# Loading the first part of a tuned matmul as float32 through SyncE, with nine warm matmuls for sixteen, and cutting k in three parts

## Chip, cores, metric

One core of one Trainium2 chip. The metric is device time in microseconds of one execution; the median of several executions is quoted. The profile's *span* runs from the first to the last instruction and is 1.7 to 3.0 us shorter than the time of the same execution, so spans are compared with spans and times with times.

## The reference

```python
m, k, n = 4096, 4096, 4096          # a, b, bias: float32, normal
return np.tanh(np.matmul(a, b) + bias)
```

## The kernel before

A and B are float32 in HBM, and TensorE multiplies float16. GpSimd's DMA queue casts on the way in. The output has four column blocks of 1024. For each row tile of 128 and column half of 512, TensorE adds up 32 k tiles of 128. Nothing is loaded at the start, so the first 8 row tiles go through the first column block in two groups of four, and k is cut in parts: group 0 and then group 1 do k tiles 0 to 7, their sums are set aside in SBUF ("spill"), and then both do the rest. Until the data is there, TensorE multiplies zeros ("warm") to raise its clock: in the trace its weight loads stand 0.43 us apart up to 5.08 us, and the matmuls 0.215 us apart in the steady part.

In the code, `across` goes through the k tiles and takes all row tiles at each, `down` finishes one row tile after the other, and a "turn" transposes A. In the profile lines `nat` is A as loaded, `tp` its transposes in PSUM, `at` and `atx` the turned A of group 0 and of group 1, `an` the A that VectorE turns itself, and `ps` the sums.

```python
    WARM = 16
    ...
    for i in range(WARM):
        nc.tensor.matmul(warm, zeros[:, :P], zeros, start=i == 0, stop=i == WARM - 1)

    raw_b = spill[3].rearrange("P (t x) n -> P t (x n)", t=2)[:, ds(0, 1), :]
    load_b_low(nc.sync, raw_b, 0, 0, 1)                   # B, k tile 0: float32, SyncE
    nc.scalar.copy(b_cur[0][:, 0, :], raw_b[:, 0, :])     # rounded by ScalarE
    nat = [opool.tile([P, P, KS], fp16, name=f"nat_{m}", tag="o_sb") for m in range(G)]

    def load_nat(m):                                      # A, row tile m: cast by GpSimd's queue
        nc.gpsimd.dma_start(
            out=nat[m], in_=a[ds(m * P, P), ds(0, P * KS)].rearrange("m (x t) -> m x t", t=KS)
        )
    ...
    def turn_nat(m):
        tp = psum.tile([P, KS, P], fp16, name="tp", tag="ps")
        for t in range(KS):
            nc.tensor.transpose(tp[:, t, :], nat[m][:, :, t], ident)
        h = KS // 2
        nc.vector.tensor_copy(ats[m][:, ds(0, h), :], tp[:, ds(0, h), :])
        nc.scalar.copy(ats[m][:, ds(h, h), :], tp[:, ds(h, h), :])
    ...
    turn_nat(0)
    turn_nat(1)
    row(0, 0, 1)      # 2 matmuls: row tile 0, k tile 0, both column halves
    row(1, 0, 1)
    across(ps, (0, 1), 1, 1, 0)
    turn_nat(2)
    ...
    across(ps, range(G), 3, KS - 2 - 3, 0)
    ...
    down(ps, KS - 2, KS, put_aside0)
    ...
    group1(0, KS, put_aside1, before1)
    # then group 0 with k tiles 8 to 31, then group 1 with k tiles 8 to 31
```

Of the kernel before, what the change touches and what calls it, by code (L numbers as in the profile page):

```python
# [14 lines left out]
P = 128  # L15
Q = 4
QP = 32
NB = 512
fp32 = mybir.dt.float32
# [4 lines left out]
def kernel(  # L24
# [7 lines left out]
    nc = tc.nc  # L32
# [4 lines left out]
    KT = K // P  # L37
    MT = M // P
    NCW = 1024
    NC = N // NCW  # L40
    J = NCW // NB
    TB = 4
    G = 4
    KS = 8
    AN = 3
    WARM = 16

    singles = ctx.enter_context(tc.tile_pool(name="singles", bufs=1))
    bpool = ctx.enter_context(tc.tile_pool(name="bpool", bufs=2))
    anat = ctx.enter_context(tc.tile_pool(name="anat", bufs=AN))  # L50
# [8 lines left out]
    def new_b():  # L59
        return [  # L60
            bpool.tile([P, TB, NCW], fp16, name=f"b_{i}", tag=f"b_{i}") for i in range(KT // TB)
        ]

    def load_b_low(queue, dst, n0, t0, nt):

        src = b[ds(0, P * KS), ds(n0, NCW)].rearrange("(x t) n -> x t n", t=KS)
        queue.dma_start(out=dst, in_=src[:, ds(t0, nt), :])  # L67
# [32 lines left out]
    def load_bias(bias_bc, n0, queue):  # L100
        src = bias[ds(n0, NCW)]
        queue.dma_start(
            out=bias_bc,
            in_=bass.AP(tensor=src.tensor, offset=src.offset, ap=[[0, P], *src.ap]),
        )


    queue, live, staged = [], [0], {}

    def pump():  # L110
        while queue and (queue[0][0] is None or live[0] < AN):
            key, uses, load = queue.pop(0)
            made = load()
            if key is not None:
                live[0] += 1
                staged[key] = [made, uses]

    def want_a(key, uses, *where):
        queue.append((key, uses, lambda: load_a(*where)))

    def want(load):
        queue.append((None, 0, load))

    def turn(at, key, mb0, t0, nt):
        pump()
        transpose_a(at, staged[key][0], mb0, t0, nt)
        staged[key][1] -= 1
        if not staged[key][1]:
            live[0] -= 1
            pump()  # L130
# [6 lines left out]
    def finish(ps, addend, mi, c0, w=NB, o_sb=None, queues=(nc.sync,)):  # L137
# [17 lines left out]
    b_cur = new_b()  # L155
    spill = [
        bpool.tile([P, 4, NB], fp32, name=f"spill_{i}", tag=f"b_{i}") for i in range(2 * G * J // 4)
    ]
    ats = [atp.tile([P, KT, P], fp16, name="at") for m in range(G)] + [
        bpool.tile([P, KT, P], fp16, name=f"atx_{m}", tag=f"b_{4 + m}") for m in range(G)  # L160
    ]

    def aside(m, j):
        return spill[(m * J + j) // 4][:, (m * J + j) % 4, :]

    def put_aside0(ps, m, j):
        nc.scalar.copy(aside(m, j), ps)  # L167

    def add_bias(m, j):
        nc.vector.tensor_tensor(  # L170
            out=aside(m, j), in0=aside(m, j), in1=bias_bc[:, ts(j, NB)], op=mybir.AluOpType.add
        )

    def put_aside1(ps, m, j):
        nc.vector.tensor_tensor(  # L175
            out=aside(m, j), in0=ps, in1=bias_bc[:, ts(j, NB)], op=mybir.AluOpType.add
        )

    def end(ps, m, j):
# [2 lines left out]
    def banks():  # L182
        return [[psum.tile([P, NB], fp32, name="ps") for j in range(J)] for m in range(G)]

    def load_b_all(t0, nt):
        for q in (0, 2, 1, 3):
            load_b(b_cur, 0, t0, nt, q)

    def across(ps, ms, t0, nt, first):
        for t in range(t0, t0 + nt):  # L190
            for m in ms:
                for j in range(J):
                    mm(ps[m][j], ats[m], b_cur, t, j, t == first, False)

    def down(ps, t0, t1, done):
        for m in range(G):
            for j in range(J):
                for t in range(t0, t1):
                    mm(ps[m][j], ats[m], b_cur, t, j, False, t == t1 - 1)
                done(ps[m][j], m, j)  # L200

    def group1(t0, t1, done, before):
        for m in range(G, 2 * G):
            for j in range(J):
                ps = psum.tile([P, NB], fp32, name="ps")
                for t in range(t0, t1):
                    mm(ps, ats[m], b_cur, t, j, t == t0, t == t1 - 1)
                before(m, j)
                done(ps, m, j)
# [6 lines left out]
    warm = psum.tile([P, NB], fp32, name="ps")  # L216
    for i in range(WARM):
        nc.tensor.matmul(warm, zeros[:, :P], zeros, start=i == 0, stop=i == WARM - 1)  # L218



    raw_b = spill[3].rearrange("P (t x) n -> P t (x n)", t=2)[:, ds(0, 1), :]
    load_b_low(nc.sync, raw_b, 0, 0, 1)
    nc.scalar.copy(b_cur[0][:, 0, :], raw_b[:, 0, :])


    nat = [opool.tile([P, P, KS], fp16, name=f"nat_{m}", tag="o_sb") for m in range(G)]

    def load_nat(m):
        nc.gpsimd.dma_start(  # L230
            out=nat[m], in_=a[ds(m * P, P), ds(0, P * KS)].rearrange("m (x t) -> m x t", t=KS)
        )

    def load_b_next():
        t = b_done[0]
        b_done[0] += 1
        load_b_low(nc.gpsimd, b_cur[t // TB][:, ds(t % TB, 1), :], 0, t, 1)

    def turn_nat(m):
        tp = psum.tile([P, KS, P], fp16, name="tp", tag="ps")  # L240
        for t in range(KS):
            nc.tensor.transpose(tp[:, t, :], nat[m][:, :, t], ident)  # L242
        h = KS // 2
        nc.vector.tensor_copy(ats[m][:, ds(0, h), :], tp[:, ds(0, h), :])  # L244
        nc.scalar.copy(ats[m][:, ds(h, h), :], tp[:, ds(h, h), :])

    b_done = [1]
    load_nat(0)
    load_nat(1)
    nc.gpsimd.affine_select(  # L250
        out=ident, in_=ident, compare_op=mybir.AluOpType.is_equal, fill=0.0,
        base=0, pattern=[[-1, P]], channel_multiplier=1,
    )
    load_b_next()
    for m in (2, 3):
        load_nat(m)
        load_b_next()
    while b_done[0] < KS:
        load_b_next()
    want_a("g1a", 2, 4 * P, 2 * Q, 0, KS)  # L260
    bias_bc = biasp.tile([P, NCW], fp32, name="bias_bc")
    want(lambda: load_bias(bias_bc, 0, nc.gpsimd))
    want_a("g1b", 2, 6 * P, 2 * Q, 0, KS)
    SA = [(KS, 8), (16, 6), (22, 6), (28, 4)]
    SB = [[(8, 4), (12, 4)], [(16, 4), (20, 2)], [(22, 2), (24, 4)], [(28, 4)]]
    for (t, nt), bs in zip(SA, SB):
        want_a(("g0", t), G, 0, G * Q, t, nt)
        for u, nu in bs:
            want(lambda u=u, nu=nu: load_b_all(u, nu))
    SG = [[(KS, 12), (KS + 12, KT - KS - 12)]] + [[(KS, KT - KS)]] * (G - 1)  # L270
    for m in range(G):
        for t, nt in SG[m]:
            want_a(("g1", m, t), 1, (G + m) * P, Q, t, nt)
    todo = [(c, mi) for c in range(NC) for mi in range(MT) if (c, mi) >= (0, 2 * G)]

    ps = []

    def row(m, t0, nt):
        if len(ps) == m:
            ps.append([psum.tile([P, NB], fp32, name="ps") for j in range(J)])  # L280
        across(ps, (m,), t0, nt, 0)

    turn_nat(0)
    turn_nat(1)
    row(0, 0, 1)
    row(1, 0, 1)
    across(ps, (0, 1), 1, 1, 0)
    turn_nat(2)
    row(2, 0, 2)
    across(ps, (0, 1, 2), 2, 1, 0)  # L290
    turn_nat(3)
    row(3, 0, 3)
    across(ps, range(G), 3, KS - 2 - 3, 0)

    def turn1(m):
        turn(ats[G + m], "g1a" if m < 2 else "g1b", (m % 2) * Q, 0, KS)

    turn1(0)
    turn1(1)
    down(ps, KS - 2, KS, put_aside0)  # L300


    def turn0(i, m):
        turn(ats[m], ("g0", SA[i][0]), m * Q, *SA[i])

    def before1(m, j):
        if m < 6 and j == 0:
            turn1(m - 2)
        if m == 6:
            turn0(0, j)  # L310
        if m == 7:
            turn0(0, 2 + j)

    group1(0, KS, put_aside1, before1)


    ps = banks()
    for i, (t, nt) in enumerate(SA):
        for m in range(G):
            if i:  # L320
                turn0(i, m)
            else:
                for j in range(J):
                    add_bias(m, j)
        across(ps, range(G), t, min(t + nt, KT - TB) - t, KS)

    def turn2(m):
        for t, nt in SG[m]:
            turn(ats[G + m], ("g1", m, t), 0, t, nt)

    turn2(0)
    down(ps, KT - TB, KT, end)

# [7 lines left out]
    def new_at(i):  # L341
        at = atp.tile([P, KT, P], fp16, name="at")
        turn(at, i, 0, 0, KT)
        at_q.append(at)
# [1 line left out]
    for i in range(ahead):  # L346
        want_row(i)

    def before2(m, j):
        if j == 0 and m < 2 * G - 1:  # L350
            turn2(m + 1 - G)
        elif m == 2 * G - 1:
            new_at(j)

    group1(KS, KT, end, before2)



    bias_next = None
    for i, (c, mi) in enumerate(todo):  # L360
        if mi == 0:
            b_cur, bias_bc = b_next, bias_next
# [21 lines left out]
        for j in range(J):  # L384
# [3 lines left out]
            for h in range(halves):  # L388
                ps = psum.tile([P, w], fp32, name="ps")
# [41 lines left out]
```

## Time and profile before

| before | |
|---|---|
| time, median of 3 | 1785.98 us (1785.80 to 1786.29) |
| the profiled execution | 1788.37 us, span 1785.4 us |
| TensorE busy | 1777.4 us, all but 100% of the span |
| one matmul in the steady part | 215.4 ns |
| first real matmul; gapless from; first part of group 0 ends | 9.35; 16.55; 26.46 us |
| last matmul to end of span | 7.2 us |

Since TensorE hardly rests later (some 0.8 us in all, near 75 and 82 us), little but the first 30 us can be gained. The runs are compared by one number: where the first part of group 0 ends. What comes after it took 1758.9 us here. The lines are in the prediction.

### The profile page before, as it was taken

Reading aid. Unit: us, or ns where it says so; the run is one execution under the profiler, and the core shown is the slowest. Engines: PE = TensorE matmul, PEld = TensorE weight load, DVE = VectorE, ACT = ScalarE, POOL = GpSimd, SP = SyncE. Lnnn points to the kernel's source line nnn. Section 1 sums busy time; section 2 is a strip of 40 time slices with the busy share of each in tenths; the row PEclk is TensorE's granted clock in tenths of the full one; section 3 lists DMA queues with packets and bytes.
Section 4 is the critical chain, followed back from the end, with each engine's and each line's share of the span. In section 5 each row is a group of like instructions: output and inputs, shape, how many; then the busy total and the mean of one; then the engine's idle time right before and its main releaser. Section 6 shows DMA issues by size and latency. Waiting matters only on the chain.

```text
span 1785.4 us, 20235 instructions
## 1 busy us (share of the span) xinstructions
PE 1777.4 (100%) x8272; PEld 808.5 (45%) x8272; DVE 846.7 (47%) x546; ACT 170.1 (10%) x273; POOL 610.8 (34%) x1130
## 2 busy tenths in 40 slices
PE   9999999999999999999999999999999999999999
PEld 4444444444444444444444444444444444444444
DVE  5564454445444544445444544454444544454442
ACT  1110000000000000000000000000000000000001
POOL 5545333332443323323353333223332233323310
PEclk9999999999999999999999999999999999999999
DMA  9999897676998866666698976666766666766631
GB/s 197 191 214 222 154 159 122 118 130 116 187 156 150 155 108 114 116 121 122 106 204 152 156 138 118 115 121 106 126 116 120 111 110 115 123 114 108 116 79 41
DMA packets 208492, 238.61 MB, mean 134 GB/s; under 512 B 28304, under 2 KB 158352, under 8 KB 208400
## 3 DMA queue, kind: packets, MB, share of 16 engines
q0 software_dynamic: 170960, 169.68, 65.2%
q1 hardware_dynamic: 37152, 67.52, 10.4%
q8 instruction: 64, 1.05, 0.2%
q14 instruction: 28, 0.23, 0.0%
q10 hardware_dynamic: 288, 0.13, 0.0%
HBM read 337.64 MB, written 67.11 MB: 227 GB/s over the span
## 4 chain that ended last, share of the span: by engine, by line
PE 95%; DMA 4%; issue 0%; POOL 0%; DVE 0%; ACT 0%; DVEq 0%; POOLq 0%
PE ps L392 93%; DMA b<-in_b_dram 2%; PE ps L133 2%; DMA an<-in_a_dram 1%; DMA bias_bc<-in_bias_dram 1%; POOL nat L230 0%; POOL b L67 0%; ACT o_sb L147 0%; DVE spill L144 0%; DVE o_sb L144 0%; POOL ident L250 0%; DVEq L144 0%; DVE atx L95 0%; POOLq L250 0%; DVEq L95 0%
## 5 line engine op out<-in xcount | busy, mean ns | idle before, releaser
L392 PE MATMUL ps<-b,at 128*128 128x512 f16 x7712 | 1657.8, 378 | 0.0
L392 PEld LDWEIGHTS <-at 128*128 128x128 f16 x7712 | 754.6, 98 | 903.3
L84 POOL DMA_DIRECT2D an<-in_a_dram x1004 | 543.6, 557 | 1051.2 <-DVE at L95 923.5
L95 DVE STREAM_TRANSPOSE at<-an 128x1024 f16<-128x1024 f16 (+3 forms) x256 | 648.0, 2574 | 16.6 <-DMA an<-in_a_dram 16.6
L144 DVE TENSOR_TENSOR o_sb<-ps,bias_bc 128x512 f32<-128x512 f32 (+1 forms) x243 | 166.1, 684 | 877.1 <-PE ps L392 755.8
L147 ACT ACTIVATE o_sb<-o_sb 128x512 f32<-128x512 f32 (+1 forms) x243 | 151.6, 625 | 1504.4 <-DVE o_sb L144 1504.4
L71 POOL DMA_DIRECT2D b<-in_b_dram x100 | 54.9, 561 | 19.4 <-DMA an<-in_a_dram 8.7
L133 PE MATMUL ps<-b,at 128*128 128x512 f16 x256 | 56.4, 379 | 1.6 <-DVE at L244 1.0
L133 PE MATMUL ps<-b,atx 128*128 128x512 f16 x256 | 55.6, 379 | 0.2 <-DVE spill L144 0.2
L133 PEld LDWEIGHTS <-at 128*128 128x128 f16 x256 | 24.7, 98 | 32.0 <-DVE at L244 1.9
L133 PEld LDWEIGHTS <-atx 128*128 128x128 f16 x256 | 25.0, 98 | 30.8 <-DVE atx L95 0.5
L95 DVE STREAM_TRANSPOSE atx<-an 128x1024 f16<-128x1024 f16 (+2 forms) x9 | 21.7, 2429 | 14.1 <-DMA an<-in_a_dram 14.0
L147 ACT ACTIVATE spill<-spill 128x512 f32<-128x512 f32 x16 | 9.9, 630 | 89.3 <-DVE spill L144 89.3
L67 POOL DMA_DIRECT2D b<-in_b_dram x13 | 8.3, 647 | 25.9 <-PE ps L392 22.6
L144 DVE TENSOR_TENSOR spill<-ps,spill 128x512 f32<-128x512 f32 x16 | 10.3, 676 | 14.0 <-PE ps L133 14.0
L244 DVE COPY at<-tp 128x512 f16<-128x512 f16 x4 | 1.7, 425 | 12.8 <-PE tp L242 12.8
L218 PE MATMUL ps<-zeros 128*128 128x512 f16 x16 | 5.5, 522 | 1.3 <-DVE zeros L214 1.3
L175 DVE TENSOR_TENSOR spill<-ps,bias_bc 128x512 f32<-128x512 f32 x8 | 5.1, 657 | 0.0
L170 DVE TENSOR_TENSOR spill<-spill,bias_bc 128x512 f32<-128x512 f32 x8 | 4.9, 681 | 0.0
L167 ACT COPY spill<-ps 128x512 f32<-128x512 f32 x8 | 4.0, 624 | 6.9 <-PE ps L133 6.9
L242 PE MATMUL tp<-ident,nat 128*128 128x128 f16 x32 | 2.8, 230 | 1.3 <-DMA nat<-in_a_dram 1.3
L218 PEld LDWEIGHTS <-zeros 128*128 128x128 f16 x16 | 2.0, 128 | 4.3 <-issue 2.5
(13 smaller groups left out, 12.9 us busy)
## 6 DMA issues: line engine op xcount, KB each, us to landing
an<-in_a_dram POOLq DMA_DIRECT2D x500, 192.0 KB, 6.6
out_dram<-o_sb SPq DMA_DIRECT2D x239, 256.0 KB, 3.2
an<-in_a_dram POOLq DMA_DIRECT2D x480, 64.0 KB, 2.4
b<-in_b_dram POOLq DMA_DIRECT2D x99, 256.0 KB, 8.2
b<-in_b_dram POOLq DMA_DIRECT2D x6, 1024.0 KB, 13.6
out_dram<-spill SPq DMA_DIRECT2D x16, 256.0 KB, 8.0
bias_bc<-in_bias_dram POOLq DMA_DIRECT2D x4, 512.0 KB, 8.8
an<-in_a_dram POOLq DMA_DIRECT2D x12, 128.0 KB, 7.7
```

What stands on the lines that cost most here:

```text
L67: queue.dma_start(out=dst, in_=src[:, ds(t0, nt), :])
L71: nc.gpsimd.dma_start(out=bt[t0 // TB][ds(q * QP, QP), ds(t0 % TB, nt), :], in_=src.rearrange("(t p) n -> p t n", p=QP),)
L84: nc.gpsimd.dma_start(out=an[ds(q * QP, QP), :, ds((t - t0) * QP, n * QP)], in_=src.rearrange("(mb p) k -> p mb k", p=QP),)
L95: nc.vector.transpose(at[:, ds(t, n), :].rearrange("P t (mb p) -> P mb t p", p=QP), an[:, ds(mb0, Q), ds((t - t0) * QP, n * QP)].rearrange ...
L133: nc.tensor.matmul(ps, at[:, t, :], bt[t // TB][:, t % TB, ts(j, NB)], start=start, stop=stop)
L144: nc.vector.tensor_tensor(out=o_sb[:, piece], in0=ps[:, piece], in1=addend[:, piece], op=mybir.AluOpType.add)
L147: nc.scalar.activation(o_sb[:, piece], o_sb[:, piece], mybir.ActivationFunctionType.Tanh)
L167: nc.scalar.copy(aside(m, j), ps)
L170: nc.vector.tensor_tensor(out=aside(m, j), in0=aside(m, j), in1=bias_bc[:, ts(j, NB)], op=mybir.AluOpType.add)
L175: nc.vector.tensor_tensor(out=aside(m, j), in0=ps, in1=bias_bc[:, ts(j, NB)], op=mybir.AluOpType.add)
L218: nc.tensor.matmul(warm, zeros[:, :P], zeros, start=i == 0, stop=i == WARM - 1)
L392: nc.tensor.matmul(ps, at[:, t, :], b_cur[t // TB][:, t % TB, ds(c0, w)], start=t == 0, stop=t == KT - 1,)
```

## The change

Intent: the casting queue brings the first row of A only at 7.5 us, while a plain float32 load through SyncE lands at 4. So the whole first part of group 0 goes through SyncE: A is rounded to float16 by VectorE and then transposed by TensorE as before, B is rounded by ScalarE. The warm matmuls are cut to nine, to end when the first row is there. k is cut in three parts (0 to 7, 8 to 15, 16 to 31), so that less data is wanted at once. The diff, cut to its core:

```diff
-    WARM = 16
+    KM = 16
+    WARM = 9
@@ (cut: put_aside, add_aside and the order of the later loads)
-    raw_b = spill[3].rearrange("P (t x) n -> P t (x n)", t=2)[:, ds(0, 1), :]
-    load_b_low(nc.sync, raw_b, 0, 0, 1)
-    nc.scalar.copy(b_cur[0][:, 0, :], raw_b[:, 0, :])
+    raw_s = anat.tile([P, 2, NCW], fp32, name="raw_s", tag="an")
+    raw_a = [anat.tile([P, 2, P, KS], fp32, name=f"raw_a{i}", tag="an") for i in range(2)]
@@ (cut)
+    def load_raw_a(m):
+        nc.sync.dma_start(
+            out=raw_a[m // 2][:, m % 2, :, :],
+            in_=a[ds(m * P, P), ds(0, P * KS)].rearrange("m (x t) -> m x t", t=KS),
+        )
+
+    def load_raw_b(t):
+        load_b_low(nc.sync, raw_b(t), 0, t, 1)
+        nc.scalar.copy(b_cur[t // TB][:, t % TB, :], raw_b(t)[:, 0, :])
+
+    def round_a(m):
+        nc.vector.tensor_copy(nat[m], raw_a[m // 2][:, m % 2, :, :])
@@ turn_nat
-        h = KS // 2
-        nc.vector.tensor_copy(ats[m][:, ds(0, h), :], tp[:, ds(0, h), :])
-        nc.scalar.copy(ats[m][:, ds(h, h), :], tp[:, ds(h, h), :])
+        nc.vector.tensor_copy(ats[m][:, ds(0, KS), :], tp)
@@
+    for m, ts_ in enumerate([(0,), (1,), (), (2, 3, 4, 5, 6, 7)]):
+        load_raw_a(m)
+        for t in ts_:
+            load_raw_b(t)
@@
+    round_a(0)
     turn_nat(0)
+    row(0, 0, 1)
+    round_a(1)
     turn_nat(1)
-    row(0, 0, 1)
     row(1, 0, 1)
     across(ps, (0, 1), 1, 1, 0)
+    round_a(2)
     turn_nat(2)
+    round_a(3)
     row(2, 0, 2)
-    across(ps, (0, 1, 2), 2, 1, 0)
     turn_nat(3)
-    row(3, 0, 3)
-    across(ps, range(G), 3, KS - 2 - 3, 0)
+    row(3, 0, 2)
+    across(ps, range(G), 2, KS - 2 - 2, 0)
@@ (cut: the three parts: down, group1 and the turns of each)
```

More of the change, by code (lines that the diff above doesn't have):

```diff
@@ L164, in aside, with put_aside, add_aside @@
         return spill[(m * J + j) // 4][:, (m * J + j) % 4, :]
-    def put_aside0(ps, m, j):
+    def put_aside(ps, m, j):
         nc.scalar.copy(aside(m, j), ps)
+    def add_aside(ps, m, j):
+        nc.vector.tensor_tensor(
+            out=aside(m, j), in0=ps, in1=aside(m, j), op=mybir.AluOpType.add
+        )
     def add_bias(m, j):
@@ L171, in add_bias @@
             out=aside(m, j), in0=aside(m, j), in1=bias_bc[:, ts(j, NB)], op=mybir.AluOpType.add
-        )
-    def put_aside1(ps, m, j):
-        nc.vector.tensor_tensor(
-            out=aside(m, j), in0=ps, in1=bias_bc[:, ts(j, NB)], op=mybir.AluOpType.add
         )
@@ L218, with raw_b @@
         nc.tensor.matmul(warm, zeros[:, :P], zeros, start=i == 0, stop=i == WARM - 1)
-    raw_b = spill[3].rearrange("P (t x) n -> P t (x n)", t=2)[:, ds(0, 1), :]
-    load_b_low(nc.sync, raw_b, 0, 0, 1)
-    nc.scalar.copy(b_cur[0][:, 0, :], raw_b[:, 0, :])
+    raw_s = anat.tile([P, 2, NCW], fp32, name="raw_s", tag="an")
+    raw_a = [anat.tile([P, 2, P, KS], fp32, name=f"raw_a{i}", tag="an") for i in range(2)]
     nat = [opool.tile([P, P, KS], fp16, name=f"nat_{m}", tag="o_sb") for m in range(G)]
-    def load_nat(m):
-        nc.gpsimd.dma_start(
-            out=nat[m], in_=a[ds(m * P, P), ds(0, P * KS)].rearrange("m (x t) -> m x t", t=KS)
-        )
-    def load_b_next():
-        t = b_done[0]
-        b_done[0] += 1
-        load_b_low(nc.gpsimd, b_cur[t // TB][:, ds(t % TB, 1), :], 0, t, 1)
+    def raw_b(t):
+        if t in (4, 5):
+            return raw_s[:, ds(t - 4, 1), :]
+        return spill[t // 2].rearrange("P (t x) n -> P t (x n)", t=2)[:, ds(t % 2, 1), :]
+    def load_raw_a(m):
+        nc.sync.dma_start(
+            out=raw_a[m // 2][:, m % 2, :, :],
+            in_=a[ds(m * P, P), ds(0, P * KS)].rearrange("m (x t) -> m x t", t=KS),
+        )
+    def load_raw_b(t):
[3 more added lines that the diff above has]
+        nc.vector.tensor_copy(nat[m], raw_a[m // 2][:, m % 2, :, :])
     def turn_nat(m):
@@ L242, in turn_nat @@
             nc.tensor.transpose(tp[:, t, :], nat[m][:, :, t], ident)
-        h = KS // 2
-        nc.vector.tensor_copy(ats[m][:, ds(0, h), :], tp[:, ds(0, h), :])
-        nc.scalar.copy(ats[m][:, ds(h, h), :], tp[:, ds(h, h), :])
-    b_done = [1]
-    load_nat(0)
-    load_nat(1)
+        nc.vector.tensor_copy(ats[m][:, ds(0, KS), :], tp)
     nc.gpsimd.affine_select(
@@ L253 @@
     )
-    load_b_next()
-    for m in (2, 3):
-        load_nat(m)
-        load_b_next()
-    while b_done[0] < KS:
-        load_b_next()
-    want_a("g1a", 2, 4 * P, 2 * Q, 0, KS)
-    bias_bc = biasp.tile([P, NCW], fp32, name="bias_bc")
-    want(lambda: load_bias(bias_bc, 0, nc.gpsimd))
-    want_a("g1b", 2, 6 * P, 2 * Q, 0, KS)
-    SA = [(KS, 8), (16, 6), (22, 6), (28, 4)]
-    SB = [[(8, 4), (12, 4)], [(16, 4), (20, 2)], [(22, 2), (24, 4)], [(28, 4)]]
-    for (t, nt), bs in zip(SA, SB):
-        want_a(("g0", t), G, 0, G * Q, t, nt)
-        for u, nu in bs:
-            want(lambda u=u, nu=nu: load_b_all(u, nu))
-    SG = [[(KS, 12), (KS + 12, KT - KS - 12)]] + [[(KS, KT - KS)]] * (G - 1)
+    for m, ts_ in enumerate([(0,), (1,), (), (2, 3, 4, 5, 6, 7)]):
+        load_raw_a(m)
+        for t in ts_:
+            load_raw_b(t)
+    live[0] = AN
+    want_a("g1a", 2, 4 * P, 2 * Q, 0, KS)
+    want_a("g1b", 2, 6 * P, 2 * Q, 0, KS)
+    want_a(("g0", KS), G, 0, G * Q, KS, KM - KS)
+    for u in range(KS, KM, TB):
+        want(lambda u=u: load_b_all(u, TB))
+    want_a("g1c", 2, 4 * P, 2 * Q, KS, KM - KS)
+    want_a("g1d", 2, 6 * P, 2 * Q, KS, KM - KS)
+    bias_bc = biasp.tile([P, NCW], fp32, name="bias_bc")
+    SA = [(KM, 8), (KM + 8, 8)]
+    for t, nt in SA:
+        want_a(("g0", t), G, 0, G * Q, t, nt)
+        for u in range(t, t + nt, TB):
+            want(lambda u=u: load_b_all(u, TB))
+    want(lambda: load_bias(bias_bc, 0, nc.gpsimd))
     for m in range(G):
-        for t, nt in SG[m]:
-            want_a(("g1", m, t), 1, (G + m) * P, Q, t, nt)
+        want_a(("g1", m), 1, (G + m) * P, Q, KM, KT - KM)
     todo = [(c, mi) for c in range(NC) for mi in range(MT) if (c, mi) >= (0, 2 * G)]
@@ L281, in row, with turn1, turn0, before2 @@
         across(ps, (m,), t0, nt, 0)
+    round_a(0)
     turn_nat(0)
+    row(0, 0, 1)
+    round_a(1)
     turn_nat(1)
-    row(0, 0, 1)
     row(1, 0, 1)
     across(ps, (0, 1), 1, 1, 0)
+    round_a(2)
     turn_nat(2)
+    round_a(3)
     row(2, 0, 2)
-    across(ps, (0, 1, 2), 2, 1, 0)
     turn_nat(3)
-    row(3, 0, 3)
-    across(ps, range(G), 3, KS - 2 - 3, 0)
-    def turn1(m):
-        turn(ats[G + m], "g1a" if m < 2 else "g1b", (m % 2) * Q, 0, KS)
-    turn1(0)
-    turn1(1)
-    down(ps, KS - 2, KS, put_aside0)
-    def turn0(i, m):
-        turn(ats[m], ("g0", SA[i][0]), m * Q, *SA[i])
-    def before1(m, j):
-        if m < 6 and j == 0:
-            turn1(m - 2)
-        if m == 6:
-            turn0(0, j)
-        if m == 7:
-            turn0(0, 2 + j)
-    group1(0, KS, put_aside1, before1)
+    row(3, 0, 2)
+    across(ps, range(G), 2, KS - 2 - 2, 0)
+    def turn1(m, keys, t, nt):
+        turn(ats[G + m], keys[m // 2], (m % 2) * Q, t, nt)
+    def turn0(m, t, nt):
+        turn(ats[m], ("g0", t), m * Q, t, nt)
+    live[0] = 0
+    for m in range(G):
+        turn1(m, ("g1a", "g1b"), 0, KS)
+    down(ps, KS - 2, KS, put_aside)
+    def before1(m, j):
+        if m == G and j == 0:
+            for i in range(G):
+                turn0(i, KS, KM - KS)
+    group1(0, KS, put_aside, before1)
+    ps = banks()
+    for m in range(G):
+        turn1(m, ("g1c", "g1d"), KS, KM - KS)
+    across(ps, range(G), KS, KM - 2 - KS, KS)
+    down(ps, KM - 2, KM, add_aside)
+    def before2(m, j):
+        if m >= 2 * G - 2:
+            turn0(2 * (m - 6) + j, *SA[0])
+    group1(KS, KM, add_aside, before2)
     ps = banks()
@@ L320 @@
             if i:
-                turn0(i, m)
-            else:
-                for j in range(J):
-                    add_bias(m, j)
-        across(ps, range(G), t, min(t + nt, KT - TB) - t, KS)
+                turn0(m, t, nt)
+        across(ps, range(G), t, min(t + nt, KT - TB) - t, KM)
     def turn2(m):
-        for t, nt in SG[m]:
-            turn(ats[G + m], ("g1", m, t), 0, t, nt)
+        turn(ats[G + m], ("g1", m), 0, KM, KT - KM)
+    for m in range(2 * G):
+        for j in range(J):
+            add_bias(m, j)
     turn2(0)
@@ L347, with before3 @@
         want_row(i)
-    def before2(m, j):
+    def before3(m, j):
         if j == 0 and m < 2 * G - 1:
@@ L353, in before2 @@
             new_at(j)
-    group1(KS, KT, end, before2)
+    group1(KM, KT, end, before3)
     bias_next = None
```

## The prediction

> **What bounds the kernel now.** I read the page first, for the engine that fills the span, then TensorE's instructions in order of time over the first 90 us, then the DMA views and the other engines over the same stretch.
>
> ```profile
> PE 1777.4 (100%) x8272; PEld 808.5 (45%) x8272; DVE 846.7 (47%) x546; ACT 170.1 (10%) x273; POOL 610.8 (34%) x1130
> ...
> 82.44 41.60 PE ps L133 x192
> 124.04 1654.20 PE ps L392 x7680
> ```
>
> The first line is the page, the other two are the chain of waits that ended last (start, length, what). From 82.44 to 1778.24 us TensorE runs 7872 matmuls (the last 512 columns are cut in two) in 1695.80 us: 215.4 ns each, without a gap. All 8192 at that pace are 1764.7 us. The span is 1785.4, so only 20.7 us are not streaming. About 7.2 us of that come after the last matmul (bias, tanh and the store of the last piece), and the change doesn't touch them. The other 13.5 us lie in the first 82 us. So no change of the head can reach 2% (35.7 us).
>
> TensorE in order of time (start, length, instruction, idle time before it and what ended it):
>
> ```profile
> 1.26 5.52 PE L218 MATMUL ps<-zeros 128*128 128x512 f16 x16 [1.26 <-DVE zeros L214]
> 7.55 0.71 PE L242 MATMUL tp<-ident,nat 128*128 128x128 f16 x8 [0.78 <-DMA nat<-in_a_dram]
> ...
> 9.35 2.15 PE L133 MATMUL ps<-b,at 128*128 128x512 f16 x8
> 11.35 0.72 PE L242 MATMUL tp<-ident,nat 128*128 128x128 f16 x8
> 12.59 2.33 PE L133 MATMUL ps<-b,at 128*128 128x512 f16 x10 [0.52 <-DVE at L244]
> 14.76 0.66 PE L242 MATMUL tp<-ident,nat 128*128 128x128 f16 x8
> ...
> 16.55 9.87 PE L133 MATMUL ps<-b,at 128*128 128x512 f16 x45 [0.22 <-ACT at L245]
> 26.46 13.99 PE L133 MATMUL ps<-b,atx 128*128 128x512 f16 x64
> ```
>
> Real matmuls begin at 9.35 us; from 16.55 they are gapless; the first part of group 0 (64 matmuls, 13.8 us of work) ends at 26.46. So 12.7 of the 13.5 us are lost before 26.46. From there to 82.44, 256 matmuls (55.1 us) take 56.0: 0.8 us more in small waits. The loss early is first the software queue (A row 0 lands only at 7.5 us), then the per-row chain of transposes and copies. The copies of one row go to two engines, but one after the other: VectorE's at 8.30 for 0.42 us, ScalarE's at 8.76 for 0.59.
>
> ```profile
> 8.30 0.42 DVE L244 COPY at<-tp 128x512 f16<-128x512 f16 x1 [6.96 <-PE tp L242]
> 8.76 0.59 ACT L245 COPY at<-tp 128x512 f16<-128x512 f16 x1 [3.66 <-DVE at L244]
> ...
> 4.05 1.04 ACT L224 CAST b<-spill 128x1024 f16<-128x1024 f32 x1 [1.97 <-DMA spill<-in_b_dram]
> ...
> nat<-in_a_dram POOLq DMA_DIRECT2D x4, 256.0 KB, 7.3
> spill<-in_b_dram SPq DMA_DIRECT2D x1, 512.0 KB, 3.2
> ```
>
> The last two are the DMA view of the first 130 us: the same 512 KB of float32 source take 7.3 us through the casting queue of GpSimd (written as 256 KB of float16), and 3.2 us through SyncE. The one load that the kernel already makes in the new way (B, k tile 0) is the best evidence for the change: landed at 4.0, rounded at 5.1.
>
> **What the Trainium skill says.** "TensorE: Matmul & The Clock Gate", Back-to-back issue gap: N/2.4 + 2.5 ns, 215.8 ns at N = 512; the trace has 215.4, so the steady part is at its floor. The same page, Part 1, says that the clock starts at half and is released after a busy window of some 3.4 us that runs free of the kernel. The trace has weight loads 0.427 us apart until 5.08 us and fast ones after: released some 3.8 us after the first warm matmul. "DMA: Bandwidth & Descriptors", Queues, rings and completion order: each DMA engine takes packets in turn from the queues that have work. Between 94 and 98 us the trace agrees:
>
> ```profile
> q1 hardware_dynamic: 524, 0.95, 70.2%
> q0 software_dynamic: 494, 0.27, 46.9%
> ```
>
> Equal packets, whatever their size. "VectorE: DVE Perf Modes", The perf-mode tier table: a float32 SBUF copy runs at 2x, 1227 ns for 2048 elements. No such copy is in this trace; 1227 ns less 2048 elements at 2 per 0.96 GHz cycle leaves 0.16 us fixed, so I estimate 0.7 us for 1024 elements from that page.
>
> **The change, part by part.**
>
> *Arrivals.* SyncE sends 12 loads of 512 KB in the order A0 B0 A1 B1 A2 A3 B2 to B7. B0's packets took 0.159 us in the median (4 KB each, 8 for each engine), so 1.3 us a load. A0 lands where B0 does now, 4.0; then B0 5.3, A1 6.6, B1 7.9, A2 9.2. GpSimd's first load (group 1's A) waits for A0 and A1 to be rounded, by the built order, so it starts near 7.4 and its packets share from about 9. With one 60 ns packet for each 4 KB one, and the overlap seen at 94 to 98 us (122 ns a pair where the durations add to 146), a pair takes about 0.19 us: 1.5 us a load. So A3 10.7, B2 12.2, B3 13.8, B4 15.3, B5 16.8, B6 18.3, B7 19.8. Each B is usable 1.15 us later (rounding, 1.04).
>
> *The row chain.* WARM 9 ends at 1.26 + 9 x 0.427 = 5.1. Row 0: A0 4.0, rounded 4.75, transposes 5.1 to 5.8, one VectorE copy of 1024 columns 5.85 to 6.6 (0.7: the 0.425 of 512 plus 512 more at 2 per cycle), B0 ready 6.45, 2 matmuls. Row 1: rounding 6.65 to 7.35, transposes to 8.1, copy to 8.8, 6 matmuls to 10.1 (B1 ready 9.05). Row 2: rounded by 9.95, transposes 10.15 to 10.85, copy to 11.6, 4 matmuls to 12.5. Row 3: VectorE is free at 11.6, rounded 12.3, transposes 12.5 to 13.2, copy to 13.95. Then 4 + 48 matmuls without a gap: 14.0 + 52 x 0.2154 = 25.2. They need B4 at 18.3 (ready 16.5), B5 at 20.0 (ready 18.0), B7 at 22.0 (ready 21.0). Against 26.46 this gains 1.26 us. About half of the earlier start (first matmul 6.65, not 9.35) is given back, because rounding, transposes and copies of four rows follow each other.
>
> *Group 1 and later.* Group 1's A: 64 packets for each engine at 0.19 from 9, the rest alone from 19.2; landed near 20, turned by VectorE in 2.05 us, ready 22.4, wanted at 25.2. After it the software queue alone moves about 0.39 MB of source a microsecond (512 KB each 1.33 us in the waits of POOL near 30 us): the second half of group 1's A 22.5, group 0's second A 28, B 8 to 15 by 38 where k tile 8 is wanted at 39.0, group 1's by 43 (wanted 52.8), the A and B of the third part by 48 to 75 (wanted 66.6 to 87). Three parts ask for less at any moment than two: before, 18 MB were wanted for one stretch of 41 us. So of the 0.8 us of small waits I give back half, 0.4. Setting aside adds 16 additions of 0.67 us on VectorE, which is under half busy; they lie beside matmuls. Matmul count and the 7.2 us of the end don't move.
>
> Sum: 1785.98 - 1.26 - 0.4 = 1784.3; I add 0.1 for the one-sided risks below.
>
> **The rivals.** (1) *The clock comes late.* Nine cold matmuls are 3.8 us, barely over one window; 16 were 6.8, two windows. If the window's phase differs, the half-busy row chain may leave the clock at half until the gapless stream has filled a window. Then 12 chain matmuls cost 0.21 more each (2.5 us) and the stream some 2 us: 1787 to 1789. For it: the skill's free-running window. Against: the trace's release at 5.1 is just where nine end, as if tuned. I give it 0.2. (2) *Shared by bytes, not packets, or delayed by the software queue:* B7 at 23 to 24, phase end 27.5 to 29, total 1786.5 to 1788. For it: out stores issued at 83.07 moved nothing until 87. Against: here the SyncE queue is first, and the counts above are equal. 0.15. (3) *Group 1's A is late,* as it starts behind the raw loads: a wait at 25 us of 1 to 3 us, 1785 to 1787. Against: 2.8 us of slack. 0.1. (4) *The chain is faster than I think:* 1 us better, 1783.
>
> **Range and chances.** The main case is 1783.3 to 1785.3; the rivals pull up. Range 1782.6 to 1787.4. Faster by 2% would need 36 us where 13.5 can be had; slower by 2% needs a stall of 36 us, only from a buffer cycle that I have missed.
>
> **What would show it.** First real matmul at 6.7 us, the gapless stream from 14, group 1's first at 25.2 with no idle before it; a SyncE load each 1.3 to 1.5 us; the VectorE rounding at 0.7; no wait over 0.3 us from 25 to 90 us. A spacing of 0.43 us after 6 us is rival 1, TensorE waiting for ScalarE's B is rival 2, for atx from VectorE is rival 3. A wait for VectorE or PSUM at a part's border would make the part about three parts wrong.

## The result, and the profile after

The changed kernel took 1791.02 us (median of 4, 1789.41 to 1791.72); before took 1786.10 (median of 4, 1785.80 to 1786.29). Ratio 1.0026, 95% interval 1.0009 to 1.0044: slower, though far within 2%. The changed kernel's time is outside my range, and its own runs spread over 2.3 us where before's spread over 0.5.

TensorE in order of time in the changed kernel (start, length, instruction, idle time before it and what ended it):

```profile
1.26 4.02 PE L219 MATMUL ps<-zeros 128*128 128x512 f16 x9 [1.26 <-DVE zeros L215]
5.08 0.95 PE L249 MATMUL tp<-ident,nat 128*128 128x128 f16 x8
6.81 0.60 PE L134 MATMUL ps<-b,at 128*128 128x512 f16 x2 [0.79 <-DVE at L250]
8.86 0.90 PE L249 MATMUL tp<-ident,nat 128*128 128x128 f16 x8 [1.44 <-DVE nat L244]
10.54 2.74 PE L134 MATMUL ps<-b,at 128*128 128x512 f16 x6 [0.79 <-DVE at L250]
13.08 1.06 PE L249 MATMUL tp<-ident,nat 128*128 128x128 f16 x8
14.92 1.89 PE L134 MATMUL ps<-b,at 128*128 128x512 f16 x4 [0.79 <-DVE at L250]
16.60 1.06 PE L249 MATMUL tp<-ident,nat 128*128 128x128 f16 x8
18.45 13.55 PE L134 MATMUL ps<-b,at 128*128 128x512 f16 x52 [0.79 <-DVE at L250]
31.83 13.98 PE L134 MATMUL ps<-b,atx 128*128 128x512 f16 x64
```

The first real matmul comes at 6.81, as predicted (6.65), 2.5 us before the old one. Then it goes wrong: six matmuls take 2.74 us, four take 1.89 (0.43 us each and not 0.215), row 1's transposes wait 1.44 us for VectorE's rounding, and the stream begins at 18.45 and not at 14.0. The first part ends at 31.83, where before had 26.46. After that no line has a wait, and the rest takes 1789.9 - 31.83 = 1758.1 us.

The clock changes that the traces record lie in steps of 3.41 us: the two ends of a stretch are two such steps apart in e1, three in e10 and four here. The same kernel in windows of that length, with the clock changes at their edges (window, its length, TensorE busy and instructions, granted clock, DMA share, GB/s):

```profile
2.37:5.78 3.41, 3.41 (x14) 1.00 0.97 358
5.78:9.19 3.41, 1.19 (x11) 1.00 1.02 364
9.19:12.60 3.41, 2.62 (x12) 0.50 1.02 401
...
16.02:19.43 3.41, 2.62 (x13) 0.50 1.13 354
19.43:22.84 3.41, 3.41 (x10) 0.50 1.39 210
```

The clock was released at 5.78, behind a full window. The next window held 1.19 us of work of 3.41 (35%), and at its end the clock went back to half, for four windows, 13.65 us, until one was full again. (The records begin with the first release. The column says 1.00 ahead of it too, where the 0.43 us spacing shows half.) Before's window behind its release was twice as full, because sixteen warm matmuls still ran in it:

```profile
5.12:8.53 3.41, 2.37 (x16) 1.00 1.02 160
```

VectorE's rounding of A rows 0 and 1 in the changed kernel:

```profile
4.30 0.69 DVE L244 CAST nat<-raw_a 128x1024 f16<-128x1024 f32 x1 [2.96 <-DMA raw_a<-in_a_dram]
8.11 0.69 DVE L244 CAST nat<-raw_a 128x1024 f16<-128x1024 f32 x1 [1.35 <-DMA raw_a<-in_a_dram]
```

A rounding is 0.69 us, as estimated. But A row 1 landed at 8.1 and not 6.6, though its load was issued at 1.73.

So there were two suspects: the clock, and the loads with the serial row chain. They were set against each other first.

### The profile page after: what moved, and what is told of

Read it like the earlier page. It is cut to its first block, busy times and chain, and to the rows that moved or that the text cites. A ratio compares the mean times of both kernels' runs of the same rounds, so it can differ in the third digit from the quotient of the medians. Undisturbed runs are those within 1.5% of the kernel's fastest.

```text
span 1789.9 us, 20279 instructions
## 1 busy us (share of the span) xinstructions
PE 1780.5 (99%) x8265; PEld 809.9 (45%) x8265; DVE 860.9 (48%) x565; ACT 180.0 (10%) x284; POOL 601.9 (34%) x1115
## 3 DMA queue, kind: packets, MB, share of 16 engines
q1 hardware_dynamic: 38736, 73.29, 11.2%
## 4 chain that ended last, share of the span: by engine, by line
PE 99%; DMA 0%; DVE 0%; issue 0%; ACT 0%; SPq 0%; DVEq 0%
PE ps L408 92%; PE ps L134 6%; DMA raw_a<-in_a_dram 0%; PE tp L249 0%; DVE at L250 0%; ACT o_sb L148 0%; DVE nat L244 0%; DVE o_sb L145 0%; SPq L68 0%; SPq L234 0%; DVEq L145 0%
## 5 line engine op out<-in xcount | busy, mean ns | idle before, releaser
L96 DVE STREAM_TRANSPOSE at<-an 128x1024 f16<-128x1024 f16 x252 | 647.5, 2610 | 1.4 <-DMA an<-in_a_dram 1.4
L72 POOL DMA_DIRECT2D b<-in_b_dram x96 | 52.3, 550 | 15.7 <-DMA an<-in_a_dram 11.7
L96 DVE STREAM_TRANSPOSE atx<-an 128x1024 f16<-128x1024 f16 (+1 forms) x12 | 21.7, 1840 | 12.6 <-DMA an<-in_a_dram 12.6
L145 DVE TENSOR_TENSOR spill<-ps,spill 128x512 f32<-128x512 f32 x16 | 11.0, 689 | 13.5 <-PE ps L134 13.5
L171 DVE TENSOR_TENSOR spill<-ps,spill 128x512 f32<-128x512 f32 x16 | 10.2, 675 | 10.3 <-issue 7.2
L68 POOL DMA_DIRECT2D b<-in_b_dram x6 | 4.5, 751 | 22.9 <-PE ps L408 22.6
L176 DVE TENSOR_TENSOR spill<-spill,bias_bc 128x512 f32<-128x512 f32 x16 | 9.7, 682 | 2.0 <-DMA bias_bc<-in_bias_dram 2.0
L168 ACT COPY spill<-ps 128x512 f32<-128x512 f32 x16 | 8.7, 605 | 14.8 <-PE ps L134 14.8
L241 ACT CAST b<-spill 128x1024 f16<-128x1024 f32 x6 | 6.3, 1046 | 11.2 <-DMA spill<-in_b_dram 11.2
```

The lines of the kernel that those rows point to most:

```text
L68: queue.dma_start(out=dst, in_=src[:, ds(t0, nt), :])
L72: nc.gpsimd.dma_start(out=bt[t0 // TB][ds(q * QP, QP), ds(t0 % TB, nt), :], in_=src.rearrange("(t p) n -> p t n", p=QP),)
L96: nc.vector.transpose(at[:, ds(t, n), :].rearrange("P t (mb p) -> P mb t p", p=QP), an[:, ds(mb0, Q), ds((t - t0) * QP, n * QP)].rearrange ...
L145: nc.vector.tensor_tensor(out=o_sb[:, piece], in0=ps[:, piece], in1=addend[:, piece], op=mybir.AluOpType.add)
L168: nc.scalar.copy(aside(m, j), ps)
L171: nc.vector.tensor_tensor(out=aside(m, j), in0=ps, in1=aside(m, j), op=mybir.AluOpType.add)
```

## The experiments

Fourteen runs were made, three of them repeats of before and of the changed kernel, all with the right result. Times are medians of five executions beside nine of before on the same chip, unless a single look is named. The record marks all timed executions as fast, that is, not disturbed; the single looks at before (e8, e14) are of unknown state and are used for their profiles alone.

### e1: sixteen warm matmuls again

```diff
-    WARM = 9
+    WARM = 16
```

> The changed kernel with 16 warm matmuls again in place of 9, nothing else. Theory 1 (the clock): 16 cold matmuls are 6.8 us, two whole windows, so at least one window is fully busy, and with row 0 turned later the next window is busier too: the clock is not taken back near 9 us; the row chain runs at full speed, the first part of group 0 ends at 26 to 27.5 us instead of 31.8, and the time is 1785 to 1787. Theory 2 (the late loads and the serial row chain): the clock is a bystander, the first part ends at 30 us or later and the time stays at 1789 to 1792.

1787.80 us (1786.75 to 1788.49), before 1786.38 (1785.68 to 1787.77), ratio 1.0005 (0.9992 to 1.0019). In its profile the first part ended at 28.6, between the two theories. The clock, released at 4.09, held for two windows, was lost at 10.92 behind one that was 43% busy, and came back at 14.33.

```profile
7.50:10.92 3.42, 1.46 (x11) 1.00 1.01 363
```

So more warm matmuls help, by 3.2 us against the changed kernel's first median and 1.6 against its second (e10, on another chip), but only push the loss back: they don't fill the windows in which the rows arrive.

### e2: nine warm matmuls in the kernel before

```diff
-    WARM = 16
+    WARM = 9
```

> The kernel before with 9 warm matmuls in place of 16, nothing else. Theory 1: the loss comes from too little TensorE work in the first windows whatever the loads are, so this kernel also loses the clock for one to four windows of 3.4 us and costs 1 to 5 us more than before, with runs spread over 1 us or more. Theory 2: no change, 1786 within 0.5 us.

1787.60 us (1786.34 to 1788.45), the same nine runs of before, ratio 1.0006 (0.9993 to 1.0018). The timing alone is not clear of noise. Its profile is clear: before's loads, and yet the clock is lost, behind a window 49% busy, for one window.

```profile
4.89:8.30 3.41, 1.68 (x18) 1.00 1.03 167
8.30:11.71 3.41, 3.41 (x12) 0.50 1.08 193
```

So the clock can be lost without the new loads. What that costs, this run doesn't show: the profiled execution was the fastest of the five (1786.34), and its first part ended at 26.39, among before's. The three slowest executions have a recorded clock of 1.000 and no profile; why they were slow stays open (a late first release, as in e11, would not lower that number).

### e3: idle matmuls in the waits

```diff
+    def fill(n):
+        idle = psum.tile([P, NB], fp32, name="ps")
+        for i in range(n):
+            nc.tensor.matmul(idle, zeros[:, :P], zeros, start=i == 0, stop=i == n - 1)
     turn_nat(0)
+    fill(3)
     row(0, 0, 1)
+    fill(5)
     round_a(1)
     turn_nat(1)
+    fill(3)
```

and three more behind the transposes of row 2 and of row 3.

> The changed kernel, still 9 warm matmuls, with 17 idle matmuls on zeros put where TensorE waits in the row chain (3 behind each row's transposes, 5 behind row 0's two matmuls); they add work and no data. Theory 1: the clock stays up from near 5.8 us, the spacing is 0.215 us from then on, the gapless stream begins near 15.5, the first part ends near 27 us even with A row 1 as late as it was, and the time is 1784.5 to 1786.5. Theory 2: the idle matmuls are only more work in a chain that waits for loads: no better than 1791, or worse by up to 3 us.

1786.82 us (1786.62 to 1787.07), ratio 1.0003 (0.9990 to 1.0015). Seventeen matmuls more, 4.2 us less than the changed kernel's first median and 2.6 less than its second (e10, on another chip), and the narrowest spread: 0.45 us. It is 0.3 us over what theory 1 gave for the time. The clock stayed up from its release on. TensorE in order of time:

```profile
9.39 0.71 PE L249 MATMUL tp<-ident,nat 128*128 128x128 f16 x8 [0.72 <-DVE nat L244]
...
10.89 1.47 PE L134 MATMUL ps<-b,at 128*128 128x512 f16 x6
...
15.95 11.40 PE L134 MATMUL ps<-b,at 128*128 128x512 f16 x52
27.19 13.98 PE L134 MATMUL ps<-b,atx 128*128 128x512 f16 x64
```

Six matmuls take 1.47 us now. The first part ends at 27.19, 4.6 us before the changed kernel's. It is still 2.0 behind my 25.2: A row 1 landed at 8.6 here. That is the second cause. The steps behind row 1, from its transposes on, take 2.80, 2.32, 1.44 and 11.24 us here, which are the prediction's 2.8, 2.35, 1.5 and 11.2.

### e4: three parts alone

The kernel before with its own loads and 16 warm matmuls, and the changed kernel's parts, setting aside and order of the later loads; the head's lines are untouched.

> The kernel before with its own loads, casts and 16 warm matmuls, but with three parts of k. My prediction gave 0.4 us to the third part; the trace of the changed kernel shows no wait at all from its first gapless matmul on, where before had 0.8 us more than its matmuls take. Theory: 0.4 to 0.9 us faster than before (1785.2 to 1785.7), with 256 matmuls from the end of the first part on taking 55.2 us and not 56.0. Rival: the third part costs time at its borders (bank releases, additions), so no gain or 0.5 us slower.

1786.04 us (1785.59 to 1788.11), ratio 1.0000 (0.9987 to 1.0012). The time can't tell 0.4 us. In the profile the rest behind the first part took 1785.5 - 27.24 = 1758.3 us without a wait, against 1758.9, 1758.7 and 1758.9 in the three profiles of before. By these profiles the third part is worth 0.4 to 0.6 us, and costs nothing.

### e5: A row 1 second in the queue

```diff
-    for m, ts_ in enumerate([(0,), (1,), (), (2, 3, 4, 5, 6, 7)]):
+    for m, ts_ in enumerate([(), (0,), (), (1, 2, 3, 4, 5, 6, 7)]):
```

on e3, with TensorE's order to match: rows 0 and 1 are turned first, then nine idle matmuls, then their two matmuls each on k tile 0; k tile 1 of rows 0 and 1 stands behind row 3's transposes. There are 15 idle matmuls (3, 9 and 3) and not 17.

> The kernel with idle matmuls (e3), with SyncE's loads reordered to A0 A1 B0 A2 A3 B1 to B7 and TensorE's work put in the matching order. It asks why A row 1 landed at 8.1 to 8.6 us where I had 6.6. Theory P (place in the queue: one DMA engine loses about a microsecond on packets sent near 5 us, so whatever is third lands late): A1, now second, is rounded near 5.6 us, and B0, now third, is rounded only at 8.2 to 8.8. Theory T (the tensor: rows of A are slow to read on this queue): A1 is late again, past 6.5, and B0 follows at 1.3 us. Under P the gapless stream starts near 14 with 54 matmuls left, but B 7 is not rounded before 23, so the first part ends at 26 to 26.7 us and the time is 0.4 to 1 us under e3's; under T no better than e3.

1786.18 us (1786.15 to 1786.66), before 1786.21 (1785.32 to 1786.89), ratio 1.0002 (0.9988 to 1.0015). A row 1 was rounded at 6.70, as soon as VectorE was free, and B's k tile 0, now third, at 7.68. The trace has 16 landing signals for each load: row 1's last came at 5.82 here (8.08 in the changed kernel), and k tile 0's 15th at 7.08 and last at 7.66. So the late signal goes with the third place, or its moment, and not with the tensor. It came earlier than theory P had it, and it doesn't always come: in e6 and e7 the third load was in by 6.94. The first part ended at 26.18, as expected; the time is 0.6 under e3's, each on its own chip.

### e6: group 1's A held back

```diff
+    held = singles.tile([P, 1], fp16, name="held")
+    nc.gpsimd.tensor_copy(held, b_cur[1][:, 0, ds(0, 1)])
     live[0] = AN
     want_a("g1a", 2, 4 * P, 2 * Q, 0, KS)
```

on e3: GpSimd sends group 1's A only when B's k tile 4 is rounded.

> The kernel with idle matmuls (e3), and one more GpSimd instruction that reads B k tile 4 after its rounding, so that group 1's A loads are sent near 17.5 us and not from 9 on. It tells what the sharing of the DMA engines costs. Theory: SyncE's loads keep 1.4 us each to the end, B 7 is rounded by 22 and not 23.5 us; the stream starts at 15.95 as before and needed B 7 only at 24, so the first part ends at 27.2 as in e3 and the time is e3's within 0.3 us, if group 1's A still comes by 27; if it comes late, TensorE waits for VectorE's atx at 27 us, by up to 2 us.

1786.25 us (1786.02 to 1787.08), ratio 1.0002 (0.9989 to 1.0014). The loads went at 1.28 us each to the end (ScalarE's roundings stand 1.28 apart), and B's k tile 7 was rounded at 19.6 where e3 had 23.5. Here A row 1 was in time (rounded at 6.96, when VectorE was free), so the stream began at 14.95 and the first part ended at 26.19: 1 us better than I wrote, for a reason that I had not written. e11 holds the loads in the same way and has A row 1 at 7.96, so the hold by itself doesn't bring it early.

### e7: e5 and e6 together

> Both of the last two. If A1's place frees the row chain and the held loads free B 7, the first part ends at 25.5 to 26 us, 1.2 to 1.7 us before e3's 27.2, and the time is 1785 to 1785.8, under before's. If group 1's A comes late, the gain is lost in a wait at 26 us. If A1 is late for another reason, no better than e3.

1786.03 us (1785.66 to 1786.60), ratio 1.0000 (0.9988 to 1.0013); first part at 26.03. Less than expected: the nine idle matmuls ran to 9.95 us and held up real ones that were ready at 8.9.

### e8 and e14: before, looked at again

> The kernel before, unchanged, for a second profile. The first one came from an execution of 1788.4 us where the timed ones have 1786, and e4, with the same loads, showed A row 0 landing at 8.5 and not 7.5 us. If the software queue's start varies from execution to execution, A row 0 lands between 5.7 and 8.6 us here too, the first part ends at 25.5 to 27.3 and the 256 matmuls after it take 55.2 to 56.0 us. If the first profile was typical, the same numbers return within 0.2 us.

> The kernel before, a third profile. Its first had A row 0 turned from 7.55 us, the first part ended at 26.46, span 1785.4; its second 6.23, 25.27 and 1784.0. I expect 5.7 to 8.6, 25.2 to 26.5 and 1783.9 to 1785.5.

| profile of before | time | span | row 0's transposes from | first part ends | the rest |
|---|---|---|---|---|---|
| first | 1788.37 | 1785.4 | 7.55 | 26.46 | 1758.9 |
| e8 | 1786.94 | 1784.0 | 6.23 | 25.27 | 1758.7 |
| e14 | 1786.83 | 1784.8 | 7.52 | 25.93 | 1758.9 |

The end of before's first part varies by 1.2 us over these three executions, and the profile that I predicted from came from the latest of the three.

### e9: a shorter fill

e7 with `fill(4)` for `fill(9)`.

> e7 with 4 idle matmuls behind row 1's transposes in place of 9. In e7 the nine ran to 9.95 us and held back row 0's first matmul, whose B was rounded at 8.0 and whose turned A was ready near 8.9. Theory (the row chain is what sets the start of the stream, and the clock stays up because its windows stay over 60% busy): the stream of 58 begins near 12.4 and not 13.4, the first part ends near 25 and not 26.0, group 1's A is turned just in time (25.6, it was in e7), so 0.4 to 1 us better than e7: 1785.1 to 1785.7. Rival: the shorter fill loses the clock near 8 or 9 us: 1787 or more.

1786.05 us (1785.38 to 1786.44), before 1785.87 (1785.13 to 1786.84), ratio 1.0001 (0.9988 to 1.0013). The stream began at 12.34, as expected, and the first part was done at 25.0. Then 1.06 us were lost. The profile puts that wait down to ScalarE:

```profile
22.03 4.01 ACT L168 COPY spill<-ps 128x512 f32<-128x512 f32 x8 [2.07 <-PE ps L134]
...
23.99 7.77 DVE L96 STREAM_TRANSPOSE atx<-an 128x1024 f16<-128x1024 f16 x4 [10.94 <-DMA an<-in_a_dram]
...
26.07 4.00 PEld L134 LDWEIGHTS <-atx 128*128 128x128 f16 x20 [1.55 <-DVE atx L96]
26.08 4.27 PE L134 MATMUL ps<-b,atx 128*128 128x512 f16 x19 [1.06 <-ACT spill L168]
```

ScalarE's eighth copy ended at 26.04, so by time it could be the releaser. But VectorE's four turns began at 23.99 when the loads landed, about 1.94 us each, and the first was done near 26 as well, and the weight load of the same moment (the third line) is put down to it. My reading was that the wait is group 1's A; e13 tests it.

### e10: the changed kernel again

> The changed kernel, unchanged, on the chip of the other runs of this call. If the windows' phase against the kernel's start is what varies, the time is again 1789 to 1792 with a spread of 1 us or more, in steps that go with whole windows at half clock; A row 1 lands between 6.9 and 8.6 us.

1789.40 us (1787.95 to 1790.90), ratio 1.0019 (1.0006 to 1.0031), beside the runs of before of e9. Its profile had the clock released at 3.95, kept behind a window 59% busy, lost at 10.78 behind one 48% busy, for three windows.

### e11: group 1's A held, no idle matmuls

The three lines of e6 on the changed kernel.

> The changed kernel (9 warm matmuls, no idle ones) with group 1's A loads held back as in e6. Theory 1 (the clock explains most of the loss): the window after the release still holds only row 0's work, 35 to 50% busy, so the clock falls again and the time stays at 1788 to 1791 although the loads are as early as in e6. Theory 2 (the loads explain it): with A row 1 at 7 us and B 7 at 19.6, the time falls to e6's 1786.3.

1788.28 us (1786.61 to 1791.73), ratio 1.0016 (1.0004 to 1.0029): theory 1 in the time, with a spread of 5 us. But the clock was not lost in its profile: it was first released at 13.80 us. The window's phase was such that the nine warm matmuls, 4.02 us, filled no window:

```profile
0.15:3.56 3.41, 2.29 (x6) 1.00 0.46 141
3.56:6.97 3.41, 2.80 (x13) 1.00 0.97 380
```

67% and 82% busy, and neither released it; of the latter's 82%, transposes alone make up 31, and the matmuls cover 51%. The window that did release it:

```profile
10.39:13.80 3.41, 3.23 (x13) 1.00 1.02 406
```

The record has the mean granted clock of every execution, also of those without a profile. For the fourteen of the changed kernel, with the hold or without (the result, e10, e11), it goes with the time: at 0.996 four took 1790.9 to 1791.7 us, at 0.997 five took 1789.4 to 1790.4, at 0.999 three took 1787.5 to 1788.0, and at 1.000 two took 1786.6 and 1788.3, the latter being the late release above. So the spread follows the clock as well.

### e12: one fill

The changed kernel with `fill(8)` behind `row(0, 0, 1)` and no other.

> The changed kernel with idle matmuls at one place only: 8 behind row 0's two matmuls. From the windows of the runs so far: the clock was lost after windows with TensorE busy 35, 43 and 49%, kept after 56% and more, and raised only by windows of 83% and more, not by 77%. Theory: 8 more matmuls of 0.215 us lift the window after the release from 35% to 70 to 85%, the next ones (rows 1 and 2, at full clock) hold 45 to 60% and are near the edge: the time is 1786.5 to 1788.5, between e3 and the changed kernel, with a wider spread than e3.

1786.94 us (1786.47 to 1788.79), ratio 1.0008 (0.9994 to 1.0022). The windows behind the release were 77, 77 and 54% busy and the clock held; one run of five was 1.7 us above the next. This is the cleanest test of the clock: one edit, on e10's chip, 2.5 us less in the medians (the ranges overlap), although A row 1 came later (8.02) than in e10's profile (7.61). One well placed fill recovers most of the loss. The last of the three windows:

```profile
12.20:15.61 3.41, 1.84 (x15) 1.00 1.10 368
```

### e13: the hold shortened

```diff
-    nc.gpsimd.tensor_copy(held, b_cur[1][:, 0, ds(0, 1)])
+    nc.gpsimd.tensor_copy(held, b_cur[0][:, 1, ds(0, 1)])
```

on e9: GpSimd waits for B's k tile 1 and no longer for tile 4.

> e9 with GpSimd waiting for B k tile 1 and not 4 before it sends group 1's A: sent near 12.4 us and not 16.9. If the wait of 1.06 us at 25 us was group 1's A, it is gone or under 0.3 us, the first part still ends at 25.0 to 25.4 us, and the time is 0.7 to 1 us under e9's in the same chip's terms: 0.4 to 1 us under before. If it was ScalarE setting aside, the wait stays at 1 us. If the earlier loads share the engines again, B 7 is rounded at 21 to 22 us and not 20, still in time.

1784.82 us (1784.66 to 1785.25), before 1785.86 (1785.34 to 1786.49), ratio 0.9995 (0.9982 to 1.0009). By the interval it is the same; but each of its five runs is below each of before's nine, by 1.0 us in the medians, and so is each span (1782.8 to 1783.4 against 1783.6 to 1784.8). TensorE, VectorE and ScalarE in order of time:

```profile
12.15 12.78 PE L134 MATMUL ps<-b,at 128*128 128x512 f16 x58
24.77 13.98 PE L134 MATMUL ps<-b,atx 128*128 128x512 f16 x64
```

```profile
22.51 8.04 DVE L96 STREAM_TRANSPOSE atx<-an 128x1024 f16<-128x1024 f16 x4 [9.46 <-DMA an<-in_a_dram]
...
21.95 4.01 ACT L168 COPY spill<-ps 128x512 f32<-128x512 f32 x8 [1.58 <-PE ps L134]
```

The turn begins 1.5 us earlier and the wait is gone, while ScalarE's eight copies still end behind TensorE's start on group 1, at 25.96 against 24.77. So e9's wait was group 1's A. Span 1782.8 us, the least of all.

## Why the prediction was wrong

**The step that failed: the row chain at full clock, behind nine warm matmuls.** I wrote that the release at 5.1 us "is just where nine end, as if tuned", and gave the late clock 0.2. I had looked only at whether the clock would be released, and not at whether the next window would be full enough to keep it. In my own times TensorE is busy for 0.7 (transposes), 0.4 (two matmuls) and 0.75 us (transposes) of the 3.4 from 5.1 to 8.5, 55%, where before's profile shows 2.37 us. By the shares measured since (lost after 49% and less, kept after 54% and more) that was on the edge even with every load on time; with row 1 late it was 35%. In the changed kernel the clock fell back for 13.65 us. The sum of its profile, against my times: row 1's transposes 1.5 us late (the load); from there to row 2's transposes 4.22 us in place of 2.8; on to row 3's 3.52 in place of 2.35; on to the stream 1.85 in place of 1.5; the stream 13.4 in place of 11.2. That is 1.5 us for the load and 5.1 for the clock: 25.2 becomes 31.8. e3 shows the clock's part by itself: with idle matmuls the last four steps take what I had written, and the first part ends 4.6 us earlier although row 1 is 0.5 us later still. e12 shows it in the time on one chip, and e2 that a loss of the clock needs none of the new loads.

**Rival 1 was nearest, but with another course and too small.** It had the clock released late. That is e11's profile: release at 13.80, 1788.28 us, inside the rival's 1787 to 1789. In the changed kernel the clock was released in time, at 5.78, and taken back at 9.19. The rival counted some 4.5 us for the clock, where it was 5.1, and took the loads as on time. The measured 1791 has both.

**Arrivals: the rate was right, two places wrong.** 1.3 us a load alone holds (1.28 in e6). The third load was not in order: predicted 6.6, in the profiles of the original order A row 1 was rounded at 6.96 once and else at 7.6 to 8.6. In e5 it is B that is late as the third. The trace shows why in part: of row 1's 16 landing signals in the changed kernel 13 came by 6.83 us, the last at 8.08; in e6 all came by 6.94. From 4.5 to 6 us a 4 KB packet took 183 ns on average in the changed kernel and 225 in e3, against 166 in e6, with single ones up to 1.25 us in e3. What makes these packets slow stays open. And group 1's A did not share the DMA engines from 9 us: issued at 9.11, its first packets went at 13.06. The sharing that followed was packet by packet, as assumed; here the DMA view of 13 to 19 us in the changed kernel:

```profile
q1 hardware_dynamic: 517, 1.87, 82.6%
q0 software_dynamic: 497, 0.25, 29.7%
```

A load took some 1.68 us in it, where I had 1.5, and B's k tile 7 landed at 21.9 and not 19.8. Apart from row 1's 1.5 us, none of this cost the changed kernel time, since its slow chain wanted B later still: TensorE never waits for B there.

**The row chain's other terms were right:** rounding 0.69 (0.7), one copy of 1024 columns 0.69 (0.7), the first matmul 6.81 (6.65).

**The base was unlucky.** I counted the gain from 26.46, the end of the first part in an execution that took 1788.4 us, and took it off a median of 1785.98. Two more profiles of before have 25.27 and 25.93. So my 25.2, even if reached, was worth 0.1 to 0.7 us over these two and not 1.26.

**Three parts:** 0.4 predicted; the rest behind the first part took 1758.1 us in the changed kernel and 1758.3 in e4, against 1758.7 to 1758.9. Right, a little small.

**Rival 3,** group 1's A late, did not occur in the changed kernel but did in e9, where the hold had made these loads later and the chain had at last become fast.

**What stays open:** why one execution's time exceeds its span by 1.8 us and another's by 3.0 (1.8 in both profiles of the changed kernel; about 3, 3 and 2 in those of before), so that small differences are better read from spans; the slow packets; and the slow executions of e2.

## What to carry to other kernels

When you cut warm-up work, check every clock window up to the first gapless stretch, not just the one that raises the clock: add up TensorE's busy time in it, and fill the waits with idle matmuls that end before the real ones are ready. A faster load gains only what the chain behind it can take up; here it took four edits (fill, order, a shorter fill, a hold) until the whole change, third part included, gained some 1 us of the 1.7 hoped for, and that inside the interval. And take two or three profiles of the kernel before, when the change is worth less than its executions differ.

## What the Trainium skill lacked or had wrong

- "TensorE: Matmul & The Clock Gate", Why this matters for your kernels, tells to avoid gaps over some 3 us. That is not enough. In the changed kernel's lost window the longest wait of TensorE was 1.44 us. What sorted the windows of the 16 profiles was the busy share of a 3.41 us window, transposes included: the clock was lost after 35, 43, 48 and 49%, and kept after 54% (twice) and more. The page also tells of clocks lost through short idles, but gives no share.
- The same page, Part 4, says that transposes don't count as busy in the same way. For the release this holds here: it came after windows with 73% and more of matmuls alone, and not after 67% and less; e11's window of 82% in all, but 51% of matmuls, did not bring it, while one of 79%, all matmuls, did (e10). For keeping the clock it does not hold: a window with 27% of matmuls, 48% with transposes, lost it (e10), and one with 26%, 63% with transposes, kept it (e4). These are shares in our profiles; the rule behind them isn't shown.
- The page's free-running window (Part 1) is borne out: with the same nine warm matmuls the first release was at 3.95, 5.78 and 13.80 us in three profiles.
- The section that the prediction cites for 215.8 ns, Back-to-back issue gap, also gives about 131 ns for a sustained stream at N = 512. Here 7872 matmuls in a row, each with its weight load, stand 215.4 ns apart.
- "DMA: Bandwidth & Descriptors", Specifications, has about 1 us to the first byte on GpSimd's queue. While SyncE's loads were still queued, the first packet went 3.9 to 4.0 us after the issue in seven runs (9.11 to 13.06 in the changed kernel, 7.69 to 11.72 in e5); with that queue nearly drained 1.45 us in four (16.40 to 17.85 in e6).
- No page: the trace's clock records begin with the first release (5.78 us in the changed kernel), and a view reads 1.00 ahead of it, while matmuls stand 0.43 us apart.
